# Gate blocks of 17 between product blocks of 16, and split tiles with a pool of their own, in the expert stage of a two-block transformer kernel

## The chip, the cores and the metric

One core of a Trainium2 chip runs the whole program. The metric is the device time of one execution in microseconds (us). The kernel before has a median of 1742.51 us over three runs (1738.4 to 1745.0).

## The reference, cut to what matters

Two transformer blocks run one after the other on 256 tokens of width 1024. The change lies at the very end of the second block, in its expert layer and the last norm:

```python
def peer_ffn(h, wq, sub_keys, u_table, v_table):
    ...
    best_v, best_pos = lax.top_k(cand, PEER_TOPK)
    expert_id = jnp.take_along_axis(cand_id, best_pos, axis=-1)
    gate = jax.nn.softmax(best_v, axis=-1)
    def block(args):
        xb, eb, gb = args
        u = jnp.take(u_table, eb, axis=0)
        act = jax.nn.gelu(jnp.einsum('phkd,pd->phk', u, xb).astype(jnp.float32), approximate=False)
        wgt = (gb * act).astype(v_table.dtype)
        return jnp.einsum('phk,phkd->pd', wgt, jnp.take(v_table, eb, axis=0))
    ...
    x = x + peer_ffn(rmsnorm_2(x, norm_ffn_w[l]), ...)
  return rmsnorm_2(x, norm_final_w)
```

There are 16384 experts (128 x 128). Every token takes 128 of them (8 heads with 16 each), and the result is x plus the gated sum of their v rows, then a root-mean-square norm with weights.

## The kernel before, in words

The kernel doesn't gather experts. It multiplies every token by the whole u table, puts the gates of the chosen experts into a dense matrix, and multiplies by the whole v table. The table has 128 groups j of 128 experts; `aw` is a tile of 128 x 128 x 256 numbers (expert in the group, group j, token) that first holds the activations and then activation times gate.

Every product of weights runs in float32r with both factors split into a high and a low part, hence three matmuls per product (hi*hi, hi*lo, lo*hi). `Weights.chunk` (its instructions are L264 to L266) fetches 512 KB of weights with one DMA on SP's queue, makes the high part on ACT (`whi<-raw`) and the low part on DVE (`wlo<-raw,whi`). Raw tiles have three buffers, high and low tiles two; in this stage every third chunk uses one more tile instead (`wpair`).

The stage around the change has three loops.

- **u steps** (`u_steps`, `u_ev`, L1170 to L1185): for each j, one chunk of the u table, 24 matmuls of 256 columns into one of four PSUM tiles (`mm`), then the evacuation. ACT takes the Gelu of the columns whose token has no gate yet straight into `aw` (L1181). For the g tokens that have a gate already it writes the Gelu to `uz` (L1184), and DVE multiplies it into `aw` (L1185).
- **gate steps** (`gates`, L1312 to L1332), 64 of them, four tokens each: DVE builds two one-hot tiles of 128 x 512 (`oa`, `ob`, L1319, two buffers each), ACT scales the four quarters of `oa` by the gate values (L1323), PE multiplies them in float32 (four matmuls into a tile `sm`, four buffers). DVE then multiplies the result into `aw` for the nu groups whose u step is done (L1329), and ACT copies it into `aw` for the other groups (L1331).
- **v steps** (L1350 to L1368): for each j, one chunk of the v table, and `split` makes the high part `wh` (ACT, L273) and the low part `wl` (DVE, L274) of `aw[:, j, :]`. 12 matmuls of 512 columns add into four PSUM accumulators `acc[t][f]` (token half t, column half f). The last two j are held back and ordered by t. Then comes the norm: Square with a row sum for both halves f, add, Sqrt, reciprocal, and one instruction per half that scales by the reciprocal and multiplies by the norm row `wnr` (L1377 to L1384).

The 24 first u steps are woven with the queries and 36 more with the top-k picks, which yield the one-hot indices. `weave(main, side, n, m)` emits n steps of main, then m of side, and so on; here it emits the remaining 68 u steps and the 64 gate steps one by one. Each engine executes its own instructions in one fixed order, which the framework derives from the order of emission, so an instruction that waits holds up all that stand behind it on that engine. `wh` and `wl` are taken from the pool `vp`, which opens after the pool `gp` (`oa`, `ob`, `uz`) has closed.

Of the kernel before, what the change touches and what calls it, by code (L numbers as in the profile page):

```python
# [3 lines left out]

# [1 line left out]

# [7 lines left out]
F32R = mybir.dt.float32r  # L14
I32 = mybir.dt.int32
U32 = mybir.dt.uint32
AF = mybir.ActivationFunctionType
# [5 lines left out]
P = 128  # L23
# [162 lines left out]
def body(tc, A, out):  # L186
# [1000 lines left out]
    with tc.tile_pool(name="sel", bufs=1) as sp_:  # L1187
# [118 lines left out]

        weave(q_steps(), u_steps(0, NU1, u_ev), 2, 3)
        weave(u_steps(NU1, NU2, u_ev), picks(), 1, 1)
    with tc.tile_pool(name="gp", bufs=1) as gpp:
        done["pool"] = gpp  # L1310

        def gates():  # L1312

            for t0 in range(0, T, 4):
                ps = psm.tile([P, 512], F32, name="sm", tag="sm")
                a = gpp.tile([P, 4, P], F32, name="oa_", tag="oa_", bufs=2)
                b = gpp.tile([P, 4, P], F32, name="ob_", tag="ob_", bufs=2)
                for o, e in ((a, eiT), (b, ejT)):
                    dve.tensor_tensor(o, iota[:, None, :].to_broadcast([P, 4, P]),  # L1319
                                      e[:, t0:t0 + 4, None].to_broadcast([P, 4, P]), OP.is_equal)  # L1320
                for q in range(4):
                    t = t0 + q
                    act.activation(a[:, q, :], a[:, q, :], AF.Copy, scale=gtT[:, t:t + 1])  # L1323
                    mm(ps[:, q * P:(q + 1) * P], a[:, q, :], b[:, q, :])
                pv = ps.rearrange("p (t j) -> p t j", t=4)
                nu = done["u"]
                done["g"] = t0 + 4
                av = aw[:, :, t0:t0 + 4].rearrange("p j t -> p t j")
                dve.tensor_tensor(av[:, :, :nu], pv[:, :, :nu], av[:, :, :nu], OP.mult)  # L1329
                if nu < NEXP:  # L1330
                    act.copy(av[:, :, nu:], pv[:, :, nu:])  # L1331
                yield  # L1332

        weave(u_steps(NU2, NEXP, u_ev), gates(), 1, 1)
    with tc.tile_pool(name="vp", bufs=1) as vp:
        h3 = cp.tile([P, KD, T], F32, name="h3", tag="uh")
        sp.dma_start(h3, hd)
        acc = [[pmm.tile([P, 512], F32, name="mm", tag="mm") for _ in range(2)] for _ in range(2)]
        wnr = vp.tile([P, D], F32, name="wnr")
        sp.dma_start(wnr, rowbc(A["rows"], 2 * P + 512, D))  # L1340
        def v_mm(j, t, w):
            wh, wl, hi, lo = w
            ah, al = wh[:, t * P:(t + 1) * P], wl[:, t * P:(t + 1) * P]
            for f in range(2):
                mm(acc[t][f], ah, hi[:, f, :], start=(j == 0), stop=False)
                mm(acc[t][f], al, hi[:, f, :], start=False, stop=False)
                mm(acc[t][f], ah, lo[:, f, :], start=False, stop=(j == NEXP - 1))

        last = []
        for j in range(NEXP):  # L1350
            hi, lo = W.chunk(A["pv"][j].rearrange("p (a b) -> p a b", a=2), (2, 512))
            wh = vp.tile([P, T], F32R, name="wh", tag="wh", bufs=3)
            wl = vp.tile([P, T], F32R, name="wl", tag="wl", bufs=3)
            split(wh, wl, aw[:, j, :])
            if j == NEXP // 2:

                act.activation(vp.tile([P, 1], F32, name="warm"), epsc, AF.Sqrt)

                for t in range(2):
                    for f in range(2):  # L1360
                        for k in range(4):
                            mm(acc[t][f][:, k * P:(k + 1) * P], h3[:, 4 * f + k, t * P:(t + 1) * P], ident,
                               start=False, stop=False)
            if j < NEXP - 2:
                for t in range(2):
                    v_mm(j, t, (wh, wl, hi, lo))
            else:
                last.append((j, (wh, wl, hi, lo)))  # L1368

        for t in range(2):  # L1370
            for j, w in last:
                v_mm(j, t, w)
            ss = vp.tile([P, 2], F32, name="fss", tag="fss", bufs=2)
            jk = vp.tile([P, 512], F32, name="fjk", tag="fjk", bufs=2)
            y = vp.tile([P, 2, 512], F32, name="y", tag="y", bufs=2)
            for f in range(2):
                act.activation(jk, acc[t][f], AF.Square, accum_out=ss[:, f:f + 1])  # L1377
            dve.tensor_tensor(ss[:, 0:1], ss[:, 0:1], ss[:, 1:2], OP.add)
            act.activation(ss[:, 0:1], ss[:, 0:1], AF.Sqrt, bias=epsc, scale=1.0 / D)
            dve.reciprocal(ss[:, 0:1], ss[:, 0:1])  # L1380
            for f in range(2):
                dve.scalar_tensor_tensor(y[:, f, :], acc[t][f], ss[:, 0:1], wnr[:, f * 512:(f + 1) * 512],
                                         OP.mult, OP.mult)
                (sp if f else act).dma_start(out[t * P:(t + 1) * P, f * 512:(f + 1) * 512], y[:, f, :])  # L1384
    ap_es.close()
    return (es,)

# [12 lines left out]
```

## Time and profile before

| what | value |
|---|---|
| median of 3 runs | 1742.51 us (1738.4 to 1745.0) |
| profiled execution, its own time | 1747.64 us |
| span of its trace, first to last instruction | 1745.9 us, 31700 instructions |
| mean granted clock | 0.990 of 2.4 GHz |
| PE busy | 1679.2 us (96%) |
| DVE busy | 1253.2 us (72%) |
| ACT busy | 1023.6 us (59%) |
| first gate matmul | 1137.01 us |
| first v product | 1385.00 us |
| last product | 1738.34 us |

PE is the matmul engine, DVE the vector engine, ACT the scalar engine; PEld are weight loads, which overlap PE. Times in the trace count from the start of the span. A matmul's recorded duration contains its way through the array, so consecutive matmuls overlap, and the pace is read from the starts. The same holds, by less than 0.1 us, for consecutive DVE and ACT instructions.

### The profile page before, as it was taken

How to read it: one execution, taken by the hardware profiler on the slowest of the kernel's cores; microseconds unless marked ns; L12 is line 12 of the kernel's file. 1: busy time of each engine (PE TensorE's matmuls, PEld its weight loads, DVE VectorE, ACT ScalarE, POOL GpSimd, SP SyncE). 2: the span in 40 equal slices, each digit the busy share in tenths (PEclk: the TensorE clock that was granted, in tenths of full speed). 3: DMA queues.
4: the chain of work that ended last, by engine and by line, in shares of the span. 5: the costliest groups of instructions: out<-in, count | busy, mean ns of one | idle time of the engine just before them, and what ended most of it. 6: DMA issues, size and time to landing. Idle time of an engine off the chain costs nothing.

```text
span 1745.9 us, 31700 instructions
## 1 busy us (share of the span) xinstructions
PE 1679.2 (96%) x12298; PEld 1575.6 (90%) x12298; DVE 1253.2 (72%) x2223; ACT 1023.6 (59%) x1977; POOL 4.0 (0%) x36
## 2 busy tenths in 40 slices
PE   2999999899999999899999999999999999999998
PEld 2998998799999999898889999999999888888886
DVE  7888677767855579757557789589999755555554
ACT  5655466565744458666645446588877544445444
POOL 0000000000000000000000000000000000000000
PEclk9999999999999999999999999999999999999999
DMA  9988689345866657216425555644444555555554
GB/s 334 342 307 312 204 291 326 122 134 184 288 205 191 182 185 234 87 38 209 142 76 191 183 180 174 203 145 146 145 135 143 190 193 195 194 174 192 195 194 138
DMA packets 97717, 336.34 MB, mean 193 GB/s; under 512 B 10988, under 2 KB 16541, under 8 KB 96926
## 3 DMA queue, kind: packets, MB, share of 16 engines
q1 hardware_dynamic: 94828, 330.63, 56.2%
q10 hardware_dynamic: 2738, 3.68, 0.6%
q8 instruction: 97, 1.59, 0.4%
q14 instruction: 54, 0.44, 0.1%
HBM read 329.02 MB, written 5.25 MB: 191 GB/s over the span
## 4 chain that ended last, share of the span: by engine, by line
PE 78%; DVE 12%; ACT 4%; issue 3%; DMA 2%; SPq 0%; DVEq 0%; ACTq 0%
PE mm L192 71%; PE sm L192 7%; DVE wlo L266 3%; DVE aw L1329 2%; ACT whi L265 1%; DMA wr<-in_w_ada 1%; DVE ac L820 1%; DVE wr L430 0%; DMA mnr<-in_rows 0%; DVE aw L1185 0%; DVE at L664 0%; DVE wpair L266 0%; DVE ul L274 0%; DMA xaV<-ke 0%; DVE ch L1285 0%
## 5 line engine op out<-in xcount | busy, mean ns | idle before, releaser
L266 DVE TENSOR_TENSOR wlo<-raw,whi 128x1024 fp32r<-128x1024 f32 (+1 forms) x448 | 543.1, 1214 | 250.5 <-ACT whi L265 249.9
L265 ACT CAST whi<-raw 128x1024 fp32r<-128x1024 f32 (+1 forms) x448 | 465.8, 1042 | 383.1 <-PE mm L192 270.1
L192 PE MATMUL mm<-uh,whi 128*128 128x256 f32 x2064 | 583.8, 285 | 9.8 <-ACT whi L265 7.4
L192 PE MATMUL mm<-ul,whi 128*128 128x256 f32 x2064 | 579.3, 281 | 2.7 <-DVE ul L274 2.2
L192 PE MATMUL mm<-uh,wlo 128*128 128x256 f32 x2064 | 578.3, 281 | 0.3 <-DVE wlo L266 0.2
L192 PEld LDWEIGHTS mm<-uh,whi 128*128 128x128 f32 x2064 | 391.4, 190 | 12.2 <-ACT whi L265 8.2
L192 PEld LDWEIGHTS mm<-ul,whi 128*128 128x128 f32 x2064 | 394.1, 191 | 4.4 <-DVE ul L274 2.7
L192 PEld LDWEIGHTS mm<-uh,wlo 128*128 128x128 f32 x2064 | 391.7, 190 | 2.1 <-DVE wlo L266 1.6
L266 DVE TENSOR_TENSOR wpair<-raw,wpair 128x1024 fp32r<-128x1024 f32 x90 | 110.2, 1224 | 80.6 <-ACT wpair L265 80.6
L192 PE MATMUL mm<-uh,wpair 128*128 128x256 f32 x768 | 143.8, 282 | 2.0 <-DVE wpair L266 1.7
L192 PE MATMUL mm<-whi,wh 128*128 128x512 f32 x344 | 134.0, 391 | 1.9 <-ACT wh L273 1.9
L192 PE MATMUL mm<-whi,wl 128*128 128x512 f32 x344 | 134.6, 391 | 0.0
L192 PE MATMUL mm<-wlo,wh 128*128 128x512 f32 x344 | 134.5, 391 | 0.0
L265 ACT CAST wpair<-raw 128x1024 fp32r<-128x1024 f32 x90 | 94.5, 1050 | 66.4 <-PE mm L192 65.3
L192 PEld LDWEIGHTS mm<-uh,wpair 128*128 128x128 f32 x768 | 119.9, 188 | 2.8 <-DVE wpair L266 2.3
L192 PE MATMUL mm<-wpair,wh 128*128 128x512 f32 x336 | 110.3, 389 | 0.0
L192 PE MATMUL mm<-ul,wpair 128*128 128x256 f32 x384 | 106.9, 278 | 0.0
L192 PE MATMUL mm<-hh,whi 128*128 128x256 f32 x352 | 99.2, 282 | 0.0
L192 PE MATMUL mm<-hl,whi 128*128 128x256 f32 x352 | 99.1, 282 | 0.0
L192 PE MATMUL mm<-hh,wlo 128*128 128x256 f32 x352 | 98.9, 281 | 0.0
L430 DVE SCALAR_TENSOR_TENSOR wr<-wr,cb 128x1024 f32<-128x1024 f32 x72 | 87.5, 1221 | 15.8 <-DMA wr<-in_w_ada 15.5
L192 PEld LDWEIGHTS mm<-whi,wh 128*128 128x128 f32 x344 | 64.6, 188 | 15.4 <-ACT wh L273 2.1
(838 smaller groups left out, 2631.7 us busy)
## 6 DMA issues: line engine op xcount, KB each, us to landing
raw<-in_pu SPq DMA_DIRECT2D x128, 512.0 KB, 3.3
raw<-in_pv SPq DMA_DIRECT2D x128, 512.0 KB, 3.3
raw<-in_ff_gu SPq DMA_DIRECT2D x88, 512.0 KB, 4.4
wr<-in_w_ada SPq DMA_DIRECT2D x72, 512.0 KB, 6.0
raw<-in_in_fm SPq DMA_DIRECT2D x34, 512.0 KB, 4.2
raw<-in_ff_dn SPq DMA_DIRECT2D x32, 512.0 KB, 3.7
raw<-in_in_tm SPq DMA_DIRECT2D x24, 512.0 KB, 4.9
raw<-in_in_gab SPq DMA_DIRECT2D x16, 512.0 KB, 3.7
```

Source lines behind the costliest of these rows:

```text
L192: pe.matmul(o, l, r, start=start, stop=stop)
L265: act.copy(hi[:, :n], raw[:, :n])
L266: dve.tensor_tensor(lo[:, :n], raw[:, :n], hi[:, :n].bitcast(F32), OP.subtract)
L430: dve.scalar_tensor_tensor(wr, wr, 1.0, cb, OP.mult, OP.mult, accum_out=mod[:, j:j + 1])
L820: dve.scalar_tensor_tensor(ac, xp[:, i:i + T], w(i), ac, OP.mult, OP.add)
L1329: dve.tensor_tensor(av[:, :, :nu], pv[:, :, :nu], av[:, :, :nu], OP.mult)
```

## The change

Four edits. `weave(..., 1, 1)` becomes `weave(islice(us, 65), gates(), 16, 17)`: 16 u steps, then 17 gate steps, and so on; three u steps come after the last gate. The tiles `wh` and `wl` get a pool `vw` that is opened before `gp`, and the splits of the first two v steps are emitted among the last three u steps. The held-back products of the last two j are ordered by column half f. In the norm DVE multiplies the accumulator by `wnr` next to each Square, and the scale by the reciprocal is done by DVE for one half and by ACT for the other.

```diff
@@ -1,6 +1,6 @@
 import math
 from contextlib import ExitStack, contextmanager
-from itertools import chain
+from itertools import chain, islice
 
 import numpy as np
 
@@ -1306,6 +1306,14 @@
 
         weave(q_steps(), u_steps(0, NU1, u_ev), 2, 3)
         weave(u_steps(NU1, NU2, u_ev), picks(), 1, 1)
+    vw = ap_es.enter_context(tc.tile_pool(name="vw", bufs=1))
+
+    def v_split(j):
+        wh = vw.tile([P, T], F32R, name="wh", tag="wh", bufs=3)
+        wl = vw.tile([P, T], F32R, name="wl", tag="wl", bufs=3)
+        split(wh, wl, aw[:, j, :])
+        return wh, wl
+
     with tc.tile_pool(name="gp", bufs=1) as gpp:
         done["pool"] = gpp
 
@@ -1331,17 +1339,23 @@
                     act.copy(av[:, :, nu:], pv[:, :, nu:])
                 yield
 
-        weave(u_steps(NU2, NEXP, u_ev), gates(), 1, 1)
+        us = u_steps(NU2, NEXP, u_ev)
+        weave(islice(us, NEXP - NU2 - 3), gates(), 16, 17)
+
+        pre = []
+        for _ in us:
+            if len(pre) < 2:
+                pre.append(v_split(len(pre)))
     with tc.tile_pool(name="vp", bufs=1) as vp:
         h3 = cp.tile([P, KD, T], F32, name="h3", tag="uh")
         sp.dma_start(h3, hd)
         acc = [[pmm.tile([P, 512], F32, name="mm", tag="mm") for _ in range(2)] for _ in range(2)]
         wnr = vp.tile([P, D], F32, name="wnr")
         sp.dma_start(wnr, rowbc(A["rows"], 2 * P + 512, D))
-        def v_mm(j, t, w):
+        def v_mm(j, t, w, fs):
             wh, wl, hi, lo = w
             ah, al = wh[:, t * P:(t + 1) * P], wl[:, t * P:(t + 1) * P]
-            for f in range(2):
+            for f in fs:
                 mm(acc[t][f], ah, hi[:, f, :], start=(j == 0), stop=False)
                 mm(acc[t][f], al, hi[:, f, :], start=False, stop=False)
                 mm(acc[t][f], ah, lo[:, f, :], start=False, stop=(j == NEXP - 1))
@@ -1349,9 +1363,7 @@
         last = []
         for j in range(NEXP):
             hi, lo = W.chunk(A["pv"][j].rearrange("p (a b) -> p a b", a=2), (2, 512))
-            wh = vp.tile([P, T], F32R, name="wh", tag="wh", bufs=3)
-            wl = vp.tile([P, T], F32R, name="wl", tag="wl", bufs=3)
-            split(wh, wl, aw[:, j, :])
+            wh, wl = pre.pop(0) if pre else v_split(j)
             if j == NEXP // 2:
 
                 act.activation(vp.tile([P, 1], F32, name="warm"), epsc, AF.Sqrt)
@@ -1363,25 +1375,29 @@
                                start=False, stop=False)
             if j < NEXP - 2:
                 for t in range(2):
-                    v_mm(j, t, (wh, wl, hi, lo))
+                    v_mm(j, t, (wh, wl, hi, lo), range(2))
             else:
                 last.append((j, (wh, wl, hi, lo)))
 
         for t in range(2):
-            for j, w in last:
-                v_mm(j, t, w)
+            for f in range(2):
+                for j, w in last:
+                    v_mm(j, t, w, (f,))
             ss = vp.tile([P, 2], F32, name="fss", tag="fss", bufs=2)
             jk = vp.tile([P, 512], F32, name="fjk", tag="fjk", bufs=2)
             y = vp.tile([P, 2, 512], F32, name="y", tag="y", bufs=2)
             for f in range(2):
                 act.activation(jk, acc[t][f], AF.Square, accum_out=ss[:, f:f + 1])
+                dve.tensor_tensor(y[:, f, :], acc[t][f], wnr[:, f * 512:(f + 1) * 512], OP.mult)
             dve.tensor_tensor(ss[:, 0:1], ss[:, 0:1], ss[:, 1:2], OP.add)
             act.activation(ss[:, 0:1], ss[:, 0:1], AF.Sqrt, bias=epsc, scale=1.0 / D)
             dve.reciprocal(ss[:, 0:1], ss[:, 0:1])
             for f in range(2):
-                dve.scalar_tensor_tensor(y[:, f, :], acc[t][f], ss[:, 0:1], wnr[:, f * 512:(f + 1) * 512],
-                                         OP.mult, OP.mult)
-                (sp if f else act).dma_start(out[t * P:(t + 1) * P, f * 512:(f + 1) * 512], y[:, f, :])
+                if f:
+                    act.activation(y[:, f, :], y[:, f, :], AF.Copy, scale=ss[:, 0:1])
+                else:
+                    dve.tensor_scalar(y[:, f, :], y[:, f, :], ss[:, 0:1], None, OP.mult)
+                (act if f else sp).dma_start(out[t * P:(t + 1) * P, f * 512:(f + 1) * 512], y[:, f, :])
     ap_es.close()
     return (es,)
 
```

What the program order of PE shows: before, each gate's four matmuls stand together with 24 products between them and the next gate's. In the changed kernel 360 more products (15 u steps) stand ahead of the first gate matmul, and then the gates come in four blocks of 17, 17, 17 and 13, with 137, 144, 144 and 96 products among them and 247, 240 and 240 products between one block and the next. The last gate's matmuls stand behind all products of the u steps, right ahead of the first v product.

DVE, the middle of the gates, one gate per u step, before (`oa`/`ob` are one-hot tiles, `aw<-sm,aw` the gate's multiply, `aw<-aw,uz` the evacuation's, `wlo`/`wpair` the low part of a chunk):

```order
L1319 TENSOR_TENSOR oa__15240<-iota,eiT 128x512
L1185 TENSOR_TENSOR aw<-aw,uz 128x120
L1329 TENSOR_TENSOR aw<-sm,aw 128x4x91
L1319 TENSOR_TENSOR ob__15241<-iota,ejT 128x512
L266 TENSOR_TENSOR wlo<-raw,whi 128x1024
L1185 TENSOR_TENSOR aw<-aw,uz 128x124
L1329 TENSOR_TENSOR aw<-sm,aw 128x4x92
L1319 TENSOR_TENSOR oa__15290<-iota,eiT 128x512
L1319 TENSOR_TENSOR ob__15291<-iota,ejT 128x512
L266 TENSOR_TENSOR wpair<-raw,wpair 128x1024
```

and in the changed kernel, from the stretch without gates into the second block:

```order
L266 TENSOR_TENSOR wlo<-raw,whi 128x1024
L1185 TENSOR_TENSOR aw<-aw,uz 128x68 x2
L1337 TENSOR_TENSOR aw<-sm,aw 128x4x92
L1327 TENSOR_TENSOR oa__14968<-iota,eiT 128x512
L1337 TENSOR_TENSOR aw<-sm,aw 128x4x92
L1327 TENSOR_TENSOR ob__14969<-iota,ejT 128x512
L1327 TENSOR_TENSOR oa__14983<-iota,eiT 128x512
L1327 TENSOR_TENSOR ob__14984<-iota,ejT 128x512
L1337 TENSOR_TENSOR aw<-sm,aw 128x4x92
L1327 TENSOR_TENSOR oa__14998<-iota,eiT 128x512
L1327 TENSOR_TENSOR ob__14999<-iota,ejT 128x512
L1337 TENSOR_TENSOR aw<-sm,aw 128x4x92
```

DVE now gets its gate work in blocks, with only the low parts of chunks and the evacuations' multiplies between them. From the first to the last multiply of each block its order holds 17 multiplies of 4x76, 29 one-hot tiles and 6 low parts; 17 of 4x92, 30 and 7; 17 of 4x108, 29 and 6; 13 of 4x124, 21 and 3.

ACT, where the u steps end and the v steps begin, before:

```order
L1184 ACTIVATE uz<-mm 128x256
L265 CAST whi<-raw 128x1024
L1184 ACTIVATE uz<-mm 128x256 x2
L265 CAST wpair<-raw 128x1024
L273 CAST wh<-aw 128x256 x3
L1357 ACT_TABLE_LOAD
```

and in the changed kernel:

```order
L1331 ACTIVATE oa__16723<-oa__16723,gtT 128x128
L265 CAST wpair<-raw 128x1024
L1331 ACTIVATE oa__16738<-oa__16738,gtT 128x128 x4
L1339 COPY aw<-sm 128x4x4 x2
L273 CAST wh<-aw 128x256 x3
L1184 ACTIVATE uz<-mm 128x256 x2
L1369 ACT_TABLE_LOAD
```

The first three casts of `wh` now stand ahead of the last two evacuations, and right behind the copies of the last two gates.

DVE, the end of the program, the changed kernel with the engine that each instruction waits for:

```order
L1391 TENSOR_TENSOR y<-mm,wnr 128x512 [waits Activation_49]
L1392 TENSOR_TENSOR fss<-fss 128x1
L1394 RECIPROCAL fss<-fss 128x1 [waits Activation_49]
L1399 TENSOR_SCALAR y<-y,fss 128x512 [waits DVE_49]
```

The multiply by the norm row waits for ACT, whose Square reads the same accumulator, and the add stands behind the multiply.

## Rows read from the trace of the kernel before

**Rows 1.** The page: busy time of each engine, share of the span, instructions.
```profile
PE 1679.2 (96%) x12298; PEld 1575.6 (90%) x12298; DVE 1253.2 (72%) x2223; ACT 1023.6 (59%) x1977; POOL 4.0 (0%) x36
```

**Rows 2.** Windows: length; busy and count by engine; granted clock; DMA share; GB/s.
```profile
1140.00:1160.00 20.00, 20.00 (x177) 20.00 (x176) 17.28 (x27) 17.74 (x45) 0.00 (x0) 1.00 0.42 145
...
1340.00:1360.00 20.00, 20.00 (x177) 20.00 (x176) 19.32 (x26) 14.12 (x43) 0.00 (x0) 1.00 0.42 140
```

**Rows 3.** Chain that ended last: u products just before the gates (start, length).
```profile
1093.18 40.84 PE mm L192 x360
```

**Rows 4.** Timeline of PE: first and third gate, next products (start, length, [idle before]).
```profile
1137.01 1.05 PE L192 MATMUL sm<-ob__13652,oa__13651 128*128 128x128 f32 x8
...
1144.36 1.06 PE L192 MATMUL sm<-ob__13751,oa__13750 128*128 128x128 f32 x8
1145.17 0.37 PE L192 MATMUL mm<-uh,whi 128*128 128x256 f32 x1
1145.37 0.28 PE L192 MATMUL mm<-ul,whi 128*128 128x256 f32 x1
```

**Rows 5.** Timeline of DVE: one gate step late in the stage.
```profile
1309.03 0.73 DVE L1319 TENSOR_TENSOR oa__16035<-iota,eiT 128x512 f32<-128x512 f32 x1
1309.63 0.73 DVE L1319 TENSOR_TENSOR ob__16036<-iota,ejT 128x512 f32<-128x512 f32 x1
1310.23 1.26 DVE L266 TENSOR_TENSOR wpair<-raw,wpair 128x1024 fp32r<-128x1024 f32 x1
1311.36 0.73 DVE L1319 TENSOR_TENSOR oa__16084<-iota,eiT 128x512 f32<-128x512 f32 x1
1312.43 0.35 DVE L1185 TENSOR_TENSOR aw<-aw,uz 128x188 f32<-128x188 f32 x1 [0.34 <-ACT uz L1184]
1312.70 1.16 DVE L1329 TENSOR_TENSOR aw<-sm,aw 128x432 f32<-128x432 f32 x1
1313.76 0.70 DVE L1319 TENSOR_TENSOR ob__16085<-iota,ejT 128x512 f32<-128x512 f32 x1
```

**Rows 6.** Timeline of DVE: the first gate's multiply and what follows it.
```profile
1138.17 0.74 DVE L1329 TENSOR_TENSOR aw<-sm,aw 128x244 f32<-128x244 f32 x1 [0.15 <-PE sm L192]
1138.82 0.69 DVE L1319 TENSOR_TENSOR oa__13750<-iota,eiT 128x512 f32<-128x512 f32 x1
```

**Rows 7.** Timeline of ACT: a gate's copy and its scaling; the first wh casts.
```profile
1355.81 0.23 ACT L1331 COPY aw<-sm 128x36 f32<-128x36 f32 x1 [1.73 <-DVE aw L1329]
1356.46 1.28 ACT L1323 ACTIVATE oa__16631<-oa__16631,gtT 128x128 f32<-128x128 f32 x4 [0.43 <-DVE oa__16631 L1319]
...
1384.55 1.02 ACT L273 CAST wh<-aw 128x256 fp32r<-128x256 f32 x3
```

**Rows 8.** Timeline of PE: the end of the u steps, the first v products.
```profile
1379.02 0.38 PE L192 MATMUL mm<-uh,wpair 128*128 128x256 f32 x1 [0.23 <-ACT wpair L265]
...
1380.28 0.50 PE L192 MATMUL mm<-uh,wpair 128*128 128x256 f32 x2 [0.76 <-DVE wpair L266]
...
1385.00 1.62 PE L192 MATMUL mm<-whi,wh 128*128 128x512 f32 x4 [1.95 <-ACT wh L273]
```

**Rows 9.** Windows, columns as in rows 2: three stretches with PE idle or just after.
```profile
340.00:350.00 10.00, 8.80 (x93) 8.39 (x92) 6.04 (x10) 5.68 (x17) 0.00 (x0) 1.00 0.38 122
700.00:710.00 10.00, 5.91 (x31) 4.83 (x31) 8.77 (x16) 6.47 (x15) 0.40 (x4) 0.82 0.63 202
1385.00:1390.00 5.00, 5.00 (x15) 3.77 (x16) 1.91 (x4) 2.61 (x5) 0.00 (x0) 0.66 1.00 385
```

**Rows 10.** Timeline of the end: last product, Square, add, the two scaled halves.
```profile
1738.34 0.39 PE L192 MATMUL mm<-wlo,wh 128*128 128x512 f32 x1
...
1738.82 0.60 ACT L1377 ACTIVATE fjk<-mm 128x512 f32<-128x512 f32 x1
...
1739.54 0.16 DVE L1378 TENSOR_TENSOR fss<-fss 128x1 f32<-128x1 f32 x1 [0.59 <-ACT fjk L1377]
...
1740.26 1.41 DVE L1382 SCALAR_TENSOR_TENSOR y<-mm,fss,wnr 128x512 f32<-128x512 f32 x2
```

## The prediction

> **What bounds the kernel now.** I read the page first: PE is busy for 96% of the span, DVE for 72% and ACT for 59% [rows 1]. Then the stage that the change touches, from the first gate at 1137.01 us [rows 4] to the first v product at 1385.00 us [rows 8], 248.0 us. In its windows PE is recorded busy in 20.00 of 20 us with the clock at 1.00 early and late; the reader should look at DVE beside it, which goes from 17.28 to 19.32 of 20 us [rows 2]. A busy PE can hide a wait, so I check by paces. Products alone run at 40.84 / 360 = 0.1134 us each [rows 3]. A gate's matmuls take 1145.17 - 1144.36 = 0.81 us, and the first product after them holds PE for 0.20 us and not 0.11, so 0.90 us in all; a step of 24 products and a gate is 2.72 + 0.90 = 3.62 us of PE. The measured step is (1144.36 - 1137.01) / 2 = 3.68 us [rows 4]: PE sets the pace.
>
> DVE is close behind. Starts give its paces: a one-hot tile 0.60 us, a chunk's low part 1.13 us, an evacuation's multiply of 188 columns 0.27 us, the gate's multiply of 432 elements 1.06 us [rows 5]; that multiply at 244 elements takes 0.65 us [rows 6], so 0.0022 us per element between. A late step costs DVE 2 x 0.60 + 1.13 + 0.27 + 1.06 = 3.66 us, as much as PE's 3.62. The even weave keeps two engines full at once, and any time in which DVE has nothing to do in this stage must show at the end.
>
> **The change, part by part.**
>
> *The dense weave* makes four blocks of gates with long product runs between. By paces, from the first to the last gate multiply of each block (counts from the order shown):
> - block 1: 17 multiplies of 304 elements at 0.78, 29 one-hot tiles, 6 low parts: 13.3 + 17.4 + 6.8 = 37.4 us
> - block 2: 17 of 368 at 0.92, 30, 7: 15.6 + 18.0 + 7.9 = 41.6 us
> - block 3: 17 of 432 at 1.06, 29, 6: 18.0 + 17.4 + 6.8 = 42.2 us
> - block 4: 13 of 496 at 1.20, 21, 3: 15.6 + 12.6 + 3.4 = 31.6 us
>
> Together 152.8 us. PE has in the same blocks 137, 144, 144 and 96 products and 64 gates: 521 x 0.1134 + 64 x 0.90 = 116.7 us. So in the blocks DVE sets the pace, and PE waits some 36 us for one-hot tiles and scaled quarters, which come behind DVE's other work. ACT has 17 scalings at 1.28 us [rows 7], 17 copies of some 0.4 us, and 6 casts per block, under 36 us: it stays below DVE.
>
> Outside the blocks it is the other way round. 360 more products stand ahead of the first gate (40.8 us), 247, 240 and 240 between the blocks (28.0, 27.2, 27.2 us). There DVE has per u step one low part and one evacuation's multiply, at most 1.5 us in PE's 2.72 us, and can't work ahead: a one-hot tile has two buffers, a low part two.
>
> At the end of a block PE needs a free `mm` tile, and the evacuations of the block's products stand in ACT's queue behind the scalings of the last gates. No row shows this wait. From below it is nothing (four tiles), from above two gates of DVE work, 2 x 2.2 = 5 us; I take 3 us, nearer to the upper end because ACT's copy waits for DVE's multiply as it does in the 1.73 us row [rows 7]. Three times that is 9 us.
>
> The first gate is then at 1137.0 + 40.8 = 1177.8 us, its multiply 1.16 us later [rows 4, 6], at 1179.0; 152.8 + 82.4 + 9 us bring the last multiply's end to 1423.2. Saved on the way: 15 evacuation multiplies, as 16 u steps now find no gate; DVE has them where it idles, so nothing.
>
> *Splits made ahead.* Now the first v product waits 1.95 us for `wh`, after waits of 0.23 and 0.76 us in the last u step [rows 8], and the clock stands at 0.66 of full speed in the 5 us after, 1.7 us lost [rows 9]. The new pool takes the reuse of `gp`'s memory out of that wait. But `wh` needs every gate, and in the new order the casts stand behind the last gate's copy. That copy comes 0.23 us after the last multiply, the first of three casts takes 0.34 us [rows 7], hand-overs 0.1 us: the first v product is at 1423.9 us, 38.9 us later than now. PE again stands still before it, so I keep the clock's loss too: nothing gained. Bounds: 2 us either way.
>
> *Last products by halves, multiply beside the Square.* The last product starts at 1738.34, the second Square follows the first at 1738.82, the add at 1739.54, and the two scaled halves run from 1740.26 to 1741.67 [rows 10]. With halves in order the first Square is long done, so the second starts some 0.06 us earlier. The order shows DVE's new multiply waiting for ACT, as both read one accumulator; a row of now has the same, where ACT's copy of a gate tile waits for DVE's multiply of it [rows 7]. At half of 1.41 us it puts 0.70 us between Square and add where 0.12 us lies now, so the add comes 0.5 us later; the two scaled halves then run on two engines, and 0.70 us of the 1.41 is saved. Sum -0.2 us. If the multiply ran beside the Square it would be -0.8, if ACT's half is slower 0. The multiplies of t = 0 lie beside t = 1's products.
>
> *Pool and queues.* SP's queue keeps the order of the chunks; a product run asks for 512 KB per 2.72 us, as the run before the gates does now without a wait [rows 3]. Nothing.
>
> **Sum:** 38.9 - 0.2 = +38.7 us. The profiled execution took 1747.64 us, 5.1 above the median of 1742.51, so the median becomes **1781 us**. About 0.5% (8.7 us) is what a measurement of this kernel can tell from no change.
>
> The Trainium skill has a rule that speaks for long product runs: "Perfetto Trace Analysis", section Matmul Optimizations, holds that matmuls should execute back-to-back in batches, because the engine scales its power with utilization. By that rule the blocks would gain or cost nothing on PE. The trace leaves it nothing to win, since the clock is at 1.00 in the even weave already [rows 2]; by the rows the sum stays.
>
> **The rivals.**
>
> *PE stays the bound, not slower.* If DVE's work in a block fits into PE's time there, the weave costs nothing: 24 products per u step and 64 gates are the same matmuls as before. Then the last gate would be ready when the u steps end, the splits would be early, and 0.23 + 0.76 + 1.95 us of waits, 1.7 us of clock and 0.2 at the end go: 1742.5 - 4.8 = 1738 us. For it: PE's windows are full now, and DVE loses 15 multiplies. Against it: it decides at block 2, where DVE would have to do 41.6 us of work in 144 x 0.1134 + 17 x 0.90 = 31.6 us, a one-hot tile in about 0.26 us where rows 5 show 0.60. Chance 0.08.
>
> *DVE is the bound in the blocks, but idles less between.* If ACT and DVE work through evacuations and low parts late in the product runs and PE doesn't notice, the 9 us go, and some 5 to 10 us more if the first gates of a block are done before PE comes to them: 1760 to 1770 us. Two buffers of one-hot tiles speak against it. Chance 0.08.
>
> *The waits in the blocks take the clock down.* Where PE was busy for 5.91 of 10 us the clock was 0.82, and after the 1.95 us wait 0.66 [rows 9]; at 8.80 of 10 us it stayed at 1.00. In block 4 PE would stand still for 9 of 31.6 us. At 1.2 GHz instead of 2.4, PE's 31.6 us of block 2 would become 63 and pass DVE's 41.6 by 21 us; if only the end of each block is slow, it is 1.7 us as at the first v product. I take 5 us for each of four blocks: 1781 + 20 = 1801 us. Chance 0.12. The Trainium skill, "TensorE: Matmul & The Clock Gate", section "HAM oscillation — how this bites in real kernels", describes a kernel whose clock swings because its matmuls come in bursts between waits; that is this rival's mechanism, and the 8.80 row is where the trace does not follow it.
>
> **How the numbers follow.** The forecast has 0.72, and its own range is 1771 (no wait at the blocks' ends, -0.8 at the end) to 1789 us (5 us at each, 2 us at the first v product). To hold 8 in 10 the range takes in the clock's typical case above and the top of the smaller loss below: 1767 to 1802 us. Slower by over 0.5% are the forecast, the clock and the smaller loss, 0.92; the rival in which PE stays the bound lies 0.3% below now, mostly within 0.5%: 0.05 same, 0.03 faster.
>
> **What would show it.** Right: the first gate near 1178 us; four stretches of 31 to 43 us in which DVE is full and PE has gaps ended by ACT's scaling or DVE's one-hot tiles; between them three stretches of 28 to 33 us with DVE half idle; the first v product near 1424 us and the same 353 us from there to the last product; the last add behind a DVE multiply. Wrong: blocks of 32 us, that is PE's own work, would mean that DVE's paces don't hold there; a granted clock under 1 inside the blocks gives the third rival; a first v product right behind the last u product would say that the splits came early.

## The result, and the profile of the changed kernel

The changed kernel takes **1796.08 us** (median of 4 runs, 1792.85 to 1797.23), the kernel before 1742.34 us in the runs beside it. The ratio is 1.0299, with an interval of 1.0274 to 1.0323: slower by 3%. The forecast was 1781, in a range of 1767 to 1802. Direction and range held; the loss was 53.7 us and not 38.7.

The pair of profiled executions shows less of it: 1747.64 us before and 1795.63 now, 48.0 us apart. The one before lay 5.30 us above the median of 1742.34, the one now 0.45 us below its own: 47.99 + 5.30 + 0.45 is the 53.74 us between the medians. The two traces are compared from here on, so the sum to be explained is the 47.7 us between their spans, 1745.9 and 1793.6.

The page, the row that answers to [rows 1]:

```profile
PE 1696.0 (95%) x12298; PEld 1586.8 (88%) x12298; DVE 1253.6 (70%) x2210; ACT 1020.1 (57%) x1964; POOL 4.1 (0%) x36
```

The same 12298 matmuls, and DVE has the same 1253 us to do in a longer span. Only PE's busy time grew by more than half a microsecond, by 16.8 us, with no matmul added: some of its records got longer. The page can't say more; the stage can.

In the chain of waits (start, length, work) the changed stage shows as long product runs, with blocks between of which the chain has only small pieces. The rows answer to [rows 3]:

```profile
1087.67 42.40 PE mm L192 x360
1130.40 43.54 PE mm L192 x384
1214.00 29.13 PE mm L192 x240
1287.35 28.90 PE mm L192 x240
...
1362.76 31.27 PE mm L192 x240
...
1431.25 354.39 PE mm L192 x1566
```

The 384 products of the second row include the 360 that were to delay the gates. Each of the three runs of 240 should take 240 x 0.1134 = 27.2 us by the pace of [rows 3]; they took 29.13, 28.90 and 31.27 us, 7.7 us too much together. The first row is a warning for small differences: its 360 products are the ones of [rows 3], which the change doesn't touch, and they took 42.40 us here and 40.84 there, a pace of 0.118 and not 0.113 us, with the clock at 1.00 in both traces.

The windows of the stage, cut at the blocks (length; busy and count by engine, PE, PEld, DVE, ACT, POOL; granted clock; DMA share; GB/s), answer to [rows 2]:

```profile
1130.00:1180.00 50.00, 49.30 (x435) 49.11 (x433) 27.08 (x28) 28.91 (x56) 0.00 (x0) 1.00 0.53 180
1180.00:1218.00 38.00, 33.27 (x260) 31.44 (x258) 37.25 (x57) 31.66 (x91) 0.00 (x0) 0.96 0.29 98
1218.00:1250.00 32.00, 31.13 (x271) 30.96 (x271) 18.62 (x28) 18.16 (x43) 0.00 (x0) 0.99 0.44 149
1250.00:1292.00 42.00, 34.16 (x258) 32.21 (x257) 39.44 (x57) 30.72 (x93) 0.00 (x0) 0.92 0.26 88
1292.00:1322.00 30.00, 28.95 (x255) 28.78 (x255) 18.02 (x25) 15.92 (x38) 0.00 (x0) 1.00 0.48 159
1322.00:1366.00 44.00, 33.01 (x256) 31.31 (x256) 43.67 (x59) 29.70 (x93) 0.00 (x0) 0.96 0.25 85
1366.00:1400.00 34.00, 32.75 (x269) 32.59 (x269) 19.11 (x26) 16.79 (x41) 0.00 (x0) 0.96 0.42 140
1400.00:1435.00 35.00, 26.04 (x172) 23.45 (x171) 32.57 (x42) 21.61 (x64) 0.00 (x0) 0.88 0.31 103
```

The reader is to look at PE and DVE in turn. In each block (second, fourth, sixth and eighth row) DVE is full, 37.25 of 38 us in the first, and PE has gaps of 5 to 11 us. In each product run PE is full and DVE has work for little more than half of the time. In the even weave both were nearly full throughout [rows 2]. Cut exactly, from the first to the last gate multiply of each block, DVE is busy for 37.21 of 37.32 us, 41.62 of 41.99, 42.61 of 42.94 and 32.12 of 33.47. The windows of the blocks also show a granted clock of 0.88 to 0.96, where the even weave had 1.00; in the exact cuts it is 1.00, 0.97, 1.00 and 0.95, so most of the low clock lies where a block ends.

Who keeps PE waiting in the stage (engine, line, what it waits for: us in total, times, longest):

```profile
PE mm L192 <- ACT uz L1184: 9.3, 4, 3.9
PE mm L192 <- ACT wh L273: 2.6, 1, 2.6
PE sm L192 <- ACT oa__15973 L1331: 2.4, 1, 2.4
```

The first row is the wait for a free `mm` tile: 2.58, 2.29 and 3.91 us at the ends of blocks 1 to 3, and 0.51 us in the first v step. The third row is the longest wait of a gate for its one-hot tile or its scaling.

PE around the end of block 3 (start, length, ..., [idle before <- what ended it]):

```profile
1356.52 1.13 PE L192 MATMUL sm<-ob__15974,oa__15973 128*128 128x128 f32 x8 [2.40 <-ACT oa__15973 L1331]
1357.72 1.13 PE L192 MATMUL sm<-ob__15989,oa__15988 128*128 128x128 f32 x8
1362.76 0.58 PE L192 MATMUL mm<-uh,whi 128*128 128x256 f32 x1 [3.91 <-ACT uz L1184]
1363.14 0.41 PE L192 MATMUL mm<-ul,whi 128*128 128x256 f32 x1
...
1368.05 0.41 PE L192 MATMUL mm<-uh,wpair 128*128 128x256 f32 x1
...
1371.26 0.28 PE L192 MATMUL mm<-uh,whi 128*128 128x256 f32 x1
1371.38 0.28 PE L192 MATMUL mm<-ul,whi 128*128 128x256 f32 x1
```

After the wait the starts lie 0.21 us apart for some 26 products, and 0.12 us apart later. This is the clock, as the windows of the wait and of just these products say; a granted clock of 0.50 is the lower level, 1.2 GHz:

```profile
1357.00:1362.00 5.00, 1.78 (x14) 1.42 (x13) 4.89 (x6) 1.93 (x8) 0.00 (x0) 1.00 0.20 63
...
1362.76:1368.50 5.74, 5.74 (x27) 5.74 (x28) 3.39 (x8) 2.58 (x10) 0.00 (x0) 0.50 0.28 93
```

So 26 x (0.213 - 0.117) = 2.5 us more, with PE recorded as busy throughout: a reader of busy shares sees nothing of it.

The ends of blocks 1 and 2 look alike:

```profile
1214.00 0.39 PE L192 MATMUL mm<-uh,wpair 128*128 128x256 f32 x1 [2.58 <-ACT uz L1184]
...
1283.18 1.88 PE L192 MATMUL sm<-ob__15179,oa__15178 128*128 128x128 f32 x8 [2.36 <-ACT oa__15178 L1331]
1287.35 0.58 PE L192 MATMUL mm<-uh,whi 128*128 128x256 f32 x1 [2.29 <-ACT uz L1184]
```

Behind block 1 some 17 products run at 0.21 us, from 1215.43 us on, and behind block 2 some 13. With block 3 that is 5.4 us of clock in the three product runs. At the ends of blocks 2 and 3 PE has two long waits in a row and not one: in block 2 the last gate's matmuls, behind a wait of 2.36 us for their scaled tile, are already slow (1.88 us where the ones of block 3 took 1.13), before the wait for a free `mm` tile begins; in block 3 the two waits are 2.40 and 3.91 us.

ACT at the end of block 3 says why PE's wait is so long, and answers to [rows 7]:

```profile
1360.97 0.30 ACT L1339 COPY aw<-sm 128x80 f32<-128x80 f32 x1 [1.79 <-DVE aw L1337]
1362.37 0.62 ACT L1184 ACTIVATE uz<-mm 128x204 f32<-128x204 f32 x2 [1.10 <-DVE aw L1185]
```

The copies of the last gates wait on ACT for DVE's multiplies, and the evacuations that would free PE's tiles stand behind them. In this block the next Gelu then waits another 1.10 us for a `uz` tile, which DVE's evacuation multiply frees.

The start of the v steps on PE, answering to [rows 8]:

```profile
1425.56 1.71 PE L192 MATMUL sm<-ob__16739,oa__16738 128*128 128x128 f32 x8
1429.88 0.86 PE L192 MATMUL mm<-whi,wh 128*128 128x512 f32 x2 [2.61 <-ACT wh L273]
1431.25 0.80 PE L192 MATMUL mm<-whi,wh 128*128 128x512 f32 x1 [0.51 <-ACT uz L1184]
1431.85 0.63 PE L192 MATMUL mm<-whi,wl 128*128 128x512 f32 x1
1432.27 0.63 PE L192 MATMUL mm<-wlo,wh 128*128 128x512 f32 x1
```

The first v product still waits, now 2.61 us, and the next ones start 0.43 us apart: the granted clock is 0.50 from 1430.34 to 1437.16 us.

The end of the program, all engines, answering to [rows 10] (ACTq is ACT's queue issuing a transfer):

```profile
1785.24 0.39 PE L192 MATMUL mm<-wlo,wh 128*128 128x512 f32 x1
...
1785.73 0.60 ACT L1390 ACTIVATE fjk<-mm 128x512 f32<-128x512 f32 x1 [0.55 <-PE mm L192]
...
1786.45 0.69 DVE L1391 TENSOR_TENSOR y<-mm,wnr 128x512 f32<-128x512 f32 x1
1787.06 1.28 ACTq L1400 DMA_DIRECT2D out<-y  x1
1787.06 0.15 DVE L1392 TENSOR_TENSOR fss<-fss 128x1 f32<-128x1 f32 x1
1788.38 0.29 ACT L1393 ACTIVATE fss<-fss,epsc 128x1 f32<-128x1 f32 x1 [1.35 <-issue]
```

DVE's multiply comes after the Square and the add after the multiply, as forecast. What was not: ACT issues a transfer of the rows done before, which takes 1.28 us, and the Sqrt stands behind it.

Where the 47.7 us lie, each stretch before and now, by the starts above and in the rows ahead:

| stretch | before | now | difference |
|---|---|---|---|
| up to the end of the picks (not touched by the change) | 1134.1 | 1130.2 | -3.9 |
| end of the picks to the first v product | 250.9 | 299.7 | +48.8 |
| first v product to the last product | 353.3 | 355.4 | +2.0 |
| last product to the end of the span | 7.6 | 8.4 | +0.8 |

Within the second row, the first gate comes 43.6 us after the picks where it came 2.9 us after them (+40.7), and from the first gate to the first v product it is 256.1 us where it was 248.0 (+8.1).

### The profile page after: what moved, and what is told of

It is laid out like the page before. It is cut to its first block, busy times and chain, and to the rows that moved or that the text cites. A ratio compares the mean times of both kernels' runs of the same rounds, so it can differ in the third digit from the quotient of the medians.

```text
span 1793.6 us, 31705 instructions
## 1 busy us (share of the span) xinstructions
PE 1696.0 (95%) x12298; PEld 1586.8 (88%) x12298; DVE 1253.6 (70%) x2210; ACT 1020.1 (57%) x1964; POOL 4.1 (0%) x36
## 4 chain that ended last, share of the span: by engine, by line
PE 63%; DVE 10%; ACT 3%; issue 2%; DMA 0%; ACTq 0%; DVEq 0%; SPq 0%
PE mm L192 58%; PE sm L192 5%; DVE aw L1337 2%; DVE wlo L266 2%; ACT whi L265 1%; DMA wr<-in_w_ada 0%; DVE wpair L266 0%; DVE ch L1285 0%; DVE ac L820 0%; DVE ul L274 0%; PE sm L1132 0%; ACT aw L1339 0%; ACT L1076 0%; DVE wr L430 0%; DVE sgb L755 0%
## 5 line engine op out<-in xcount | busy, mean ns | idle before, releaser
L192 PEld LDWEIGHTS mm<-uh,whi 128*128 128x128 f32 x2064 | 393.0, 191 | 19.1 <-ACT whi L265 8.5
```

Source lines behind the costliest of these rows:

```text
L192: pe.matmul(o, l, r, start=start, stop=stop)
```

## The experiments

**Is it the weave?** Three kernels take the change apart. The first is the changed kernel with the even weave back:

```diff
-        weave(islice(us, NEXP - NU2 - 3), gates(), 16, 17)
+        weave(islice(us, NEXP - NU2 - 3), gates(), 1, 1)
```

> The changed kernel with one gate step per u step again; the pool of its own, the early splits, the halves and the new norm tail stay. Theory A (the loss is the weave: in the blocks DVE sets the pace, outside them it idles, and PE waits): the whole loss goes, 1736 to 1744 us; the first v product follows the last u product with less than the 1.95 us wait of the kernel before, and the tail from the last product's start to the end of the span keeps the 8.4 us of the changed kernel against 7.6 before. Theory B (a fixed price at the end of every block: PE waits for a free product tile, the clock falls): the same here, as there are no blocks. Theory C (part of the loss is in the pool, the early splits or the tail): over 1750 us.

Measured: 1739.4 us, ratio to the kernel before 0.9989 (0.9975 to 1.0004). All the loss is gone. One part of the expectation failed: the end takes 7.5 us as in the kernel before, not the 8.4 us of the changed kernel, and ACT's issue in it 0.38 us. In its trace the splits made ahead do what they should; PE where the u steps end, against [rows 8]:

```profile
1379.74 0.28 PE L192 MATMUL mm<-uh,wpair 128*128 128x256 f32 x1
1379.86 0.39 PE L192 MATMUL mm<-whi,wh 128*128 128x512 f32 x1
1380.08 0.39 PE L192 MATMUL mm<-whi,wl 128*128 128x512 f32 x1
```

The first v product follows at once, without the 1.95 us wait, and at full pace. The stage is 1.6 us shorter than before and the v steps 1.8 us: 3.4 us in the trace, 0.2% of the program, which the interval can't tell from nothing. This is the best version of the study: level with the kernel before, and 3% ahead of the changed one.

The second is the kernel before with the dense weave alone:

```diff
-        weave(u_steps(NU2, NEXP, u_ev), gates(), 1, 1)
+        us = u_steps(NU2, NEXP, u_ev)
+        weave(islice(us, NEXP - NU2 - 3), gates(), 16, 17)
+        for _ in us:
+            pass
```

> The kernel before with nothing but the weave of 16 and 17. Theory A and B: 1793 to 1800 us, all of the changed kernel's loss or a little more, as the early splits are missing and the tail of before is 0.8 us shorter. Theory C: clearly under 1790 us.

Measured: 1794.1 us, ratio 1.0299 (1.0264 to 1.0335), the changed kernel's own. The first v product waits 5.81 us for `wh` here, since the splits have the old pool and place, where the changed kernel waits 2.61. So the early splits take part of the wait back even in the dense weave, too little for the time to show.

The third is the kernel before with the new order of the last products and the new norm alone:

```diff
+            for f in range(2):
+                for j, w in last:
+                    v_mm(j, t, w, (f,))
...
+                dve.tensor_tensor(y[:, f, :], acc[t][f], wnr[:, f * 512:(f + 1) * 512], OP.mult)
...
+                if f:
+                    act.activation(y[:, f, :], y[:, f, :], AF.Copy, scale=ss[:, 0:1])
+                else:
+                    dve.tensor_scalar(y[:, f, :], y[:, f, :], ss[:, 0:1], None, OP.mult)
```

> The kernel before with nothing but the last products by halves and the new norm tail. If ACT's issue of the first output half's DMA (1.28 us, standing ahead of the second Sqrt in ACT's order) is what makes the tail longer, the tail from the last product's start to the end of the span is 8.2 to 8.5 us, with an idle of over 1 us of ACT before the Sqrt; if the tail of the changed kernel was longer through something in the stage before, it is 7.4 us (the 0.2 us less that was forecast). The time is 1743 us in either case, within what a measurement can tell.

Measured: 1743.14 us in one run, which by itself says little. From the last product to the end of the span it is 7.45 us, against 7.56 before and 8.36 in the changed kernel. ACT at the end of this kernel:

```profile
1735.76 0.37 ACTq L1388 DMA_DIRECT2D out<-y  x1
1736.18 0.29 ACT L1381 ACTIVATE fss<-fss,epsc 128x1 f32<-128x1 f32 x1 [0.45 <-DVE fss L1380]
```

The issue takes 0.37 us here and is done before the Sqrt has its operand. So alone the new end is worth 0.1 us in this trace, where 0.2 us were forecast, and the 1.28 us in the changed kernel don't come from the new end by itself.

**How does it depend on the block's length?** The changed kernel with `weave(..., 4, 4)`, and with `weave(..., 8, 8)`:

> The changed kernel with blocks of 4 u steps and 4 gate steps, 16 blocks. Theory A: the front shrinks to 3 u steps ahead of the first gate (8 us, of which DVE idles 5), and the two buffered one-hot tiles, two low parts and four gate tiles smooth much of a block of four: 1748 to 1760 us. Theory B (some 6 us at every block end: 2.6 to 3.9 us of waiting for a product tile and 3 us at the low clock): 16 ends cost about 96 us, over 1800 us.

> The changed kernel with 8 u steps and 8 gate steps in turn instead of 16 and 17. The loss so far goes 0 with one and one, +12 us against the even weave in span with four and four, +54 with 16 and 17. Theory A: what counts is the time in which DVE has nothing it may do, since its one-hot tiles have two buffers: it grows with the length of the first product run and of the runs between, so eight lies between: last gate to first v without a wait, 1760 to 1785 us. Rival B: the loss comes from one threshold between 4 and 16 (a wait at the end of a block that takes the clock down), and with eight it is either not there (1745 to 1757 us) or whole (over 1788 us).

Measured: 1752.86 us with four, ratio 1.007 (1.0044 to 1.0097), and 1769.09 us with eight, ratio 1.0154 (1.012 to 1.0189). Both lie in theory A's ranges. From the end of the picks to the first v product it takes 249.3 us with one and one, 265.8 with four, 274.8 with eight and 299.7 with 16 and 17. The loss grows with the length, with no threshold among the lengths tested. In the kernels with four and eight the granted clock is 1.00 from the first gate to the first v product, so their loss is not the clock's; the first v product has no wait ahead of it and the v steps take 351.6 and 353.3 us. The first gate comes 11.4, 21.9 and 43.6 us after the picks, where it comes 2.8 us after them with one and one: 8.6, 19.1 and 40.8 us of the 16.5, 25.5 and 50.4 us that the stage lost against it.

**Is the place of the first product run at fault?** The changed kernel with the gates first:

```diff
-        weave(islice(us, NEXP - NU2 - 3), gates(), 16, 17)
+        weave(gates(), islice(us, NEXP - NU2 - 3), 17, 16)
```

> The changed kernel with 17 gate steps first and then 16 u steps, and so on, instead of 16 u steps and then 17 gate steps. The block of products that stood ahead of the first gate now stands behind the last one. Theory A: it is no matter where DVE idles; the product runs between and behind the blocks are 219, 216, 219 and 323 products, 977 in all where the changed kernel has 360 + 247 + 240 + 240 = 1087, so DVE still idles for some 95 percent as long, and the splits are early, which takes some 3 us off: 1780 to 1797 us. Rival B: the 15 u steps ahead of the first gate are the part that costs, as a delay of all gates by 41 us, and the blocks themselves fit into PE's time: with the first gate back at its old place 1748 to 1762 us.

Measured: 1783.76 us, ratio 1.0244 (1.0206 to 1.0282). The first gate is back at 2.0 us after the picks, 41.6 us sooner than in the changed kernel, and the kernel gains 12 us, not 41 (10 by the ratios to the kernel before, whose intervals overlap a little). What was taken away at the front comes back behind the last gate: it starts at 1375.90 us and the first v product at 1421.16, with products alone between. The windows of its first block, the run after it, and the end:

```profile
1131.00:1172.00 41.00, 36.21 (x284) 33.96 (x282) 39.93 (x60) 38.57 (x106) 0.00 (x0) 0.97 0.31 102
1172.00:1197.00 25.00, 24.65 (x200) 24.68 (x201) 13.28 (x25) 13.49 (x36) 0.00 (x0) 0.91 0.39 130
...
1378.00:1415.00 37.00, 35.06 (x298) 34.87 (x297) 23.38 (x34) 18.01 (x32) 0.00 (x0) 1.00 0.57 186
```

The pattern is the same, DVE full in the block and idle for some 40% of the run, the last one included. So "the first gate comes 40.7 us late" is where the loss is seen in the changed kernel, and not what causes it: products without gates leave DVE idle wherever they stand.

**Does PE have slack in the blocks?** Each gate's four matmuls are issued twice in a row, so that PE has 64 x 0.81 = 52 us more to do and no other engine anything, first in the even weave and then in the changed kernel:

```diff
                     mm(ps[:, q * P:(q + 1) * P], a[:, q, :], b[:, q, :])
+                    mm(ps[:, q * P:(q + 1) * P], a[:, q, :], b[:, q, :])
```

> The even weave (as the first experiment) with every gate's four matmuls done twice, so PE has 64 x 0.81 = 52 us more to do and no other engine has anything more. PE is full in this weave: at least 52 us more than the even weave, 1790 to 1820 us (more than 52 where the longer way from one-hot tile to free buffer holds DVE up).

> The changed kernel with every gate's four matmuls done twice, the same 52 us more of PE work. Theory A (DVE sets the pace in the blocks and PE waits some 36 us there): the added work lies mostly in PE's waits, 8 to 28 us more than the changed kernel, 1804 to 1824 us, less than half of what it costs in the even weave. Rival (PE is still what bounds the blocks, and the loss comes from somewhere else): the same 52 us or more as in the even weave, over 1845 us.

Measured: the even weave goes from 1739.4 to 1813.94 us, by 74.5; the changed kernel from 1796.08 to 1817.68 us, by 21.6 (by spans 67.1 and 21.8). In the even weave all 52 us show, and more (why more was not looked into). In the changed kernel 30 of them vanish in gaps that PE had in the blocks; that is what is meant by DVE setting the pace there. In this kernel none of PE's waits for a free `mm` tile is left, and its windows of the first two blocks, against the second and the fourth row of the changed kernel, read:

```profile
1180.00:1220.00 40.00, 38.87 (x324) 37.20 (x324) 34.67 (x52) 32.93 (x89) 0.00 (x0) 1.00 0.08 20
1250.00:1295.00 45.00, 42.96 (x352) 40.48 (x351) 40.75 (x59) 32.79 (x95) 0.00 (x0) 1.00 0.13 42
```

PE is nearly full now, and its clock stays at 1.00.

**Is it the clock that makes the product runs long?** After the last gate of blocks 1 to 3, 24 matmuls on data that lies there anyway, with a result that nobody reads, fill PE's wait:

```diff
+        def gates_fill():
+            for i, _ in enumerate(gates()):
+                if i % 17 == 16:
+                    fp = psm.tile([P, 512], F32, name="fl", tag="sm")
+                    for _ in range(24):
+                        mm(fp[:, :T], uh[:, 0, 0:P], uh[:, 0, :])
+                yield
-        weave(islice(us, NEXP - NU2 - 3), gates(), 16, 17)
+        weave(islice(us, NEXP - NU2 - 3), gates_fill(), 16, 17)
```

> The changed kernel with 24 more matmuls of 256 columns (2.7 us at 0.1134) on PE right behind the last gate of each of the first three blocks, into a tile that nobody reads. Clock theory (PE stands still 2.6 to 3.9 us there for a free product tile, the clock falls, and the some 25 products after it run at 0.21 us instead of 0.117, 2.9 us lost per block end): the added work lies in the wait, the products after it run at 0.12 us, and the time falls by 5 to 9 us below the changed kernel, to 1785 to 1791 us. Rival (the clock falls for what happened in the block before, or the price at the block ends is the wait alone): no gain, 1794 to 1799 us, or more if the added work does not fit into the wait.

Measured: 1789.78 us, ratio 1.028 (1.0247 to 1.0312). By time alone that isn't told from the changed kernel's 1.0274 to 1.0323. Its trace is plain. PE at the end of block 3:

```profile
1356.45 2.99 PE L192 MATMUL fl<-uh 128*128 128x256 f32 x23
1360.57 0.39 PE L192 MATMUL mm<-uh,whi 128*128 128x256 f32 x1 [1.13 <-ACT uz L1184]
1360.79 0.28 PE L192 MATMUL mm<-ul,whi 128*128 128x256 f32 x1
1360.91 0.28 PE L192 MATMUL mm<-uh,wlo 128*128 128x256 f32 x1
```

and the product runs after blocks 2 and 3 in its chain of waits:

```profile
1286.64 27.36 PE mm L192 x240
1360.57 27.48 PE mm L192 x240
```

Products start 0.12 us apart from the second on, the granted clock of 1356 to 1371 us is 1.00, and the runs of 240 take 27.4 and 27.5 us where the changed kernel took 28.9 and 31.3. From the first gate to the first v product it is 249.5 us, 6.6 less than in the changed kernel. That is about the clock's share, which the starts put at 5.4 us; the filler covers part of the waits too. The first v product, which has no filler ahead of it, still waits 2.31 us.

**Would more one-hot tiles let DVE work ahead?** The kernel of the dense weave alone, with four `oa` and `ob` tiles each instead of two:

> The kernel before with the weave of 16 and 17 (as the second experiment) and four buffers instead of two for each of the one-hot tiles. If the two buffers are what keeps DVE from using the product runs, two more gates' one-hot tiles (2 x 2 x 0.60 = 2.4 us) are made ahead of each of the last three blocks: 4 to 10 us less than the second experiment's 1794, with gates still in four blocks. If buffers do not matter because a gate's multiply, scaling and low parts fill the block anyway, no difference that can be measured.

Measured: 1790.36 us, ratio 1.0273 (1.0234 to 1.0313), against 1.0264 to 1.0335 with two: no difference that the time shows. The stage takes 297.4 us instead of 301.6, in one trace each, which would fit the lower edge of the first expectation; which of the two holds is not decided. With two more tiles DVE can be two gates ahead when a block starts, of 17.

## Why the prediction was right, and where it was short

The path that the forecast described is the one that the traces show; its sum was 15 us short. Its own range, 1771 to 1789 us, did not hold. The stated range did, because it had been widened to take in the clock rival at its typical size, and the clock was indeed a part of what was missing.

**The delay of the first gate: right.** 360 products were to bring it to 1177.8 us, 40.8 us later. It came 40.7 us later, counted from the end of the picks; by the start of the span it is 1173.78 us, because the untouched stages before were 3.9 us faster in this execution.

**DVE sets the pace in the blocks: right, and shown.** The windows have DVE full and PE with gaps, and the doubled gate matmuls cost 21.6 us there and 74.5 in the even weave. From the first gate of one block to that of the next, block, wait and product run together were forecast at 68.4, 71.8 and 72.4 us; measured were 69.2, 73.1 and 77.8. The blocks alone, from the first to the last gate multiply, took 37.3, 42.0, 42.9 and 33.5 us where 37.4, 41.6, 42.2 and 31.6 stood.

**The wait for a free `mm` tile: right.** 3 x 3 = 9 us were forecast from bounds of 0 and 5 (two gates at 2.2 us are 4.4); 2.58 + 2.29 + 3.91 = 8.8 us were measured, for the reason given: the evacuations stand on ACT behind copies that wait for DVE. That the sum fits so closely is in part luck, since 3 us was a choice between bounds and the longest wait has a second cause in it, the 1.10 us for a `uz` tile.

**The product runs: the term that was mis-sized.** "28.0, 27.2, 27.2 us" was worked out with the pace of PE at 2.4 GHz. The three runs of 240 took 7.7 us more than 3 x 27.2. Of these, 5.4 us are the clock: the waits at the end of a block have a second price, since PE, which had been busy for 1.78 of the 5 us from 1357 to 1362, comes out of them with the granted clock at 0.50. Another 0.9 us is the pace of 0.118 us that the third run keeps with the clock back at 1.00, as the 360 products ahead of the gates did; no run shows its cause. The clock is the third rival, which had 5 us for each of four blocks and a chance of 0.12. The mechanism was there, at a third of its size (5.4 us for the three ends where it had 15); forecast and rival were not one or the other, as the text had them, but both. The prediction weighed the section "HAM oscillation — how this bites in real kernels" of the Trainium skill, "TensorE: Matmul & The Clock Gate", against a row with 8.80 of 10 us busy at a clock of 1.00 [rows 9] and gave the row more weight. That row held for blocks 1 to 3 up to their last gates; in block 4 the clock stood at 0.50 between 1423.51 and 1426.92 us, from the end of a wait of 2.33 us for a one-hot tile on. At the ends of the blocks PE's waits are long, and there the section's picture, bursts that start slow after a wait, is what the trace shows, 2.5 us of it at block 3.

**The splits made ahead: right, against the kernel before.** Nothing was to be gained, since the casts of `wh` stand behind the last gate's copy. The first v product waits 2.61 us where it waited 1.95, and the v steps take 2.0 us longer, most of it the clock, which stands at 0.50 for 6.8 us there and for 3.4 us before. Against the dense weave without them the early splits do shorten this wait, from 5.81 us. With the even weave the same edit gains the 3.4 us that the first rival had put at 0.23 + 0.76 + 1.95 us of waits and 1.7 us of clock, of which the first two stayed.

**The end: right in the steps, short by 1 us in the sum.** -0.2 us were forecast, +0.8 measured, and -0.1 when the new end runs alone. The difference is the 1.28 us of ACT's transfer issue, a step that stands in no term of the forecast.

**The sum.** 38.7 us were forecast and 51.6 measured in the three stretches that the change touches (48.8 + 2.0 + 0.8). Of the missing 12.9 us, about 7 lie in the product runs (89.3 us measured where 82.4 stood), 5.4 of them the clock's; 2.0 lie in the v steps and 1.0 at the end. The other 3 us are in the blocks, 1.9 of them in block 4, where DVE itself stood idle for 1.35 us. The remaining 2 us up to the 53.7 between the medians are differences between executions.

**The rivals.** "PE stays the bound" (1738 us) and "DVE idles less between" (1760 to 1770 us) are out: the dense weave alone costs 3%, and even blocks of four cost 0.7%.

**What stays open.** Why ACT's transfer issue took 1.28 us; it did so in no kernel with blocks of at most eight, nor with the gates first. Why products keep a pace of 0.113 us in some runs and 0.118 in others at a clock of 1.00. And why the doubled matmuls cost 74.5 us and not 52 in the even weave.

## What to carry to other kernels

When two engines are both nearly full, an even weave of their work is worth keeping: bunching the work of one makes the other wait in the bunch, and leaves the first idle between the bunches. Two more buffers gave it too little work ahead for the time to show. Work out, for each stretch between two waits, what every engine has to do there, and take the largest; here the sum of these maxima, with the waits for `mm` tiles, came within 10 us of the 256 us from the first gate to the first v product, while the average loads (DVE 72%, PE 96%) said nothing of it. And price a long wait of PE's twice, once for its length and once for the products after it, which may run at half the clock while PE counts as busy.

## What was not expected of the hardware

- The clock's fall shows best in the distance of starts: 0.213 us between products of 256 columns at a granted clock of 0.50 and 0.113 to 0.118 us at 1.00. After PE's waits of 2.58, 2.29 and 3.91 us at the ends of blocks 1 to 3, some 17, 13 and 26 products ran at the slower pace.
- With the clock at 1.00 products of 256 columns keep one of two paces through a whole run: the same 360 products took 40.84 us in the kernel before and 42.40 in the changed one. The cause is not known, and 4% of a product run is more than some of the terms above.
- Filling the wait with 24 matmuls kept the clock at 1.00, at no cost that the trace shows, since PE had nothing else to do. Doubling PE's work in the gates did the same.
- The issue of the first output transfer on ACT's queue took 1.28, 1.21 and 1.06 us in the changed kernel and in its versions with filler and with doubled matmuls, and 0.37 to 0.38 us in the six other traces with the new end; SP's issues took 0.34 us each in all nine. In the three, a fetch of instructions on queue q14 lies 0.3 to 0.4 us ahead of that issue, and in the last 9 us of the span of the six there is none. That is a coincidence in time and was not tested.
